# First stage in another order, adaptive columns spread over both products of the first FFN, keys stored once, spills read behind middle chunks

## The chip, the cores and the metric

The kernel runs on one core of one Trainium2 chip. The metric is the device time of one execution in microseconds. Kernel and reference work in float32. On TensorE a float32 product is made of three products of rounded float32 halves, so every product of two 128-wide tiles with 512 columns is three matmuls of 128x512.

## The reference, cut to what matters

A two-block transformer with 512 tokens and width 1024. All norms are followed by a shift and a scale that come from a conditioning vector `c` (the "adaptive" columns).

```python
ada = silu(c) @ ada_w + ada_b          # shift and scale vectors of every norm
# block A
h = modulate(rms_norm(x, pre_mix_g0), shift, scale)
x = x + gate * rms(gmlp_mixer(h, w_in, ...))      # u, v = gelu(h @ w_in), v mixed over tokens
x = x + gate * rms(swiglu(modulate(rms_norm(x)), w_gu0, w_down0))
# shared keys and values
h = modulate(rms_norm(x, kv_norm_g), *mod_kv)
k, v, f = split(h @ kv_w);  k = rms_norm(k);  dcum = cumsum(log_sigmoid(f))
# block B: mixers in one residual sum
q, gate = split(modulate(rms_norm(x)) @ w_qg)
o = softmax(q k^T / 8 + dcum[t] - dcum[s], causal) v
...                                       # further mixers: indexed attention, mLSTM
x = x + gate * rms(swiglu(modulate(rms_norm(x)), w_gu1, w_down1))
```

Token embeddings `p @ w_pl` are made at the start and used later.

## The kernel before, in words

**Split operands.** `wsplit` (L272 to L281) takes a weight tile of 128x1024 (512 KB, loaded by SP into the ring `raw` of four): ACT rounds it into `whi` (L277), then DVE or POOL subtracts it to give `wlo` (L280). `share=n` gives every n-th subtraction to POOL, 0 gives all to DVE. Activations have the same two parts, `h[0]` (high) and `h[1]` (low). `mm3` (L413 to L416) issues high times high (L414), high times low or low times high (L415, L416).

**Products.** `gemm_a` (L418) makes transposed outputs, 24 matmuls to a block: the first four blocks as a group, then block by block. `gemm_b` (L457) makes outputs with tokens in the partitions, in chunks of 256 rows of weights, 24 matmuls each, over four PSUM accumulators.

**Adaptive columns.** 96 of the 112 columns of `ada` that are needed are made in the background by `fill` (L305): it loads one column as a 128x1024 tile into the `raw` ring and lets DVE multiply and sum it in one operation (L300). One loaded column is held back. In the first FFN's gate and up product (`ffn`, L590) two columns go to each block, and what is left then follows it in a `while` loop (L608). `need` (L321) makes a vector complete before its use.

**First stage** (L616 to L776). The orders of ACT, DVE, PE and SP are written by hand in one block. It rounds `pT`, makes embeddings (`embed`, a product of 6 matmuls and an evacuation at L670 to L672), the squares of `x` (L689) and the norm of two tiles at a time (`norm2`, L685), then for each of eight column groups `prep`: two adaptive columns (L300), three small DVE operations (L729 to L731), a weight split, four transposes (L382), an ACT evacuation with scale and shift (L405), a DVE cast into the high part (L406) and a DVE subtraction into the low part (L407). `products(k)` multiplies with `w_v` chunk `k//2`, and with two blocks of `w_u`. `prep(k+1)` is written ahead of `products(k)`.

**Keys and queries.** The keys of a pair of heads (128x512) are split and written to DRAM by `spread` (L938, on POOL's queue), each half of the partitions twice, so that loads find the tiles in the form in which the logits use them: four tiles of 256 KB to a pair (`kscr`). `loader` (L944) reads them back a pair ahead, four tiles to a pair. The indexed attention has six tiles to a pair in `ascr` (`ev_a`, L1284).

**Spills.** Eight transposed tiles of normed `x` are written to DRAM earlier (`xT`) and read back at L1122 to L1129: load, ACT scale and shift (L1127), DVE cast and subtraction. This loop stands ahead of the product of `w_vv`. ACT evacuates the keys of group 1 at L886 and L889 in the same stretch; `kdone(1)` then rounds and writes them.

**Gates.** `columns` (L1249) transposes `iwt` and then, at L1259, the gates `la` and `lt` of the mLSTM, in one function that runs at the first block of `w_aqk`.

Of the kernel before, what the change touches and what calls it, by code (L numbers as in the profile page):

```python
# [20 lines left out]
P = 128  # L21
# [10 lines left out]
ND = 2  # L32
LATE = 2
AHEAD = 3
PRE = 4
# [5 lines left out]
GU = (2, 3)  # L41
GG = (1, 1)
DT = (4, 4)
DS = (0, 0)
# [3 lines left out]
IG = 1  # L48
# [141 lines left out]
def body(tc, nc, a):  # L190
    V, S_, G, PE = nc.vector, nc.scalar, nc.gpsimd, nc.tensor

    with ExitStack() as es:
# [99 lines left out]
        def ada_load(col, raw=None):  # L293
# [5 lines left out]
        def ada(col, raw):  # L299
            V.scalar_tensor_tensor(raw, raw, 1.0, cact[0], ALU.mult, ALU.mult, accum_out=modc[:, col:col + 1])  # L300
# [4 lines left out]
        def fill(n=1):  # L305

            frac[0] += n
            while frac[0] >= 1:
                frac[0] -= 1
                if ada_next[0] < len(ADA):  # L310
                    held.append(ada_load(ADA[ada_next[0]]))
# [106 lines left out]
        def gemm_a(h, w, n, evac, m=P, group=0, nfill=0, share=0, gshare=1):  # L418
# [38 lines left out]
        def gemm_b(h, w, groups, kt, evac, head=False, tail=0, nfill=0, share=0, raws=(), hshare=1, then={}):  # L457
# [6 lines left out]
            for gi in groups:  # L464
# [125 lines left out]
        def ffn(l, h, xsrc, xdst, gb, nxt):  # L590
            with tc.tile_pool(name=f"f{l}", bufs=44) as pf:
# [19 lines left out]
                gemm_b((hh, hl), a[f"w_dn{l}"], range(2), KF, post(gb, xsrc, xdst, F, nxt()), tail=DT[l], share=DS[l])  # L611
# [7 lines left out]
        accs = [acc() for _ in range(NT)]  # L619
        h = hpair()  # L620
        with tc.tile_pool(name="l0", bufs=20) as p0:
# [7 lines left out]
            EVA = (0, 0)  # L629

            crow = L2()[0:1, :]
            nc.sync.dma_start(crow, a["crow"])
            pf = [L(), L()]
            wpl = []
            for k in range(2):
                nc.sync.dma_start(pf[k], a["pT"][k])
            for k in range(2):
                wpl.append(load_w(a["w_pl"][k, 0]))
            xn = {}
            for t in range(NT):  # L640
                xn[t] = [L(), L()]
                for q in range(2):
                    nc.sync.dma_start(xn[t][q], a["x"][t * P:(t + 1) * P, q * 512:(q + 1) * 512])
                if t == 1:
                    nc.sync.dma_start(vecs[:], a["vecs"])
                    nc.sync.dma_start(ident[:], a["ident"])

            relb = L()[0:32, 0:8]
            nc.sync.dma_start(relb, a["relb"])
            oneh = L2()[0:32, 0:640]  # L650
            nc.sync.dma_start(oneh, a["onehot"])
            bscr = scratch([8, 640])
            ada0, raws = {}, {}
            for k in range(PRE):
                ada0[k] = [ada_load(col, L2()) for col in (8 + k, k)]
                if k < 4:
                    raws[k] = load_w(a["w_v"][0, k // 2] if k % 2 == 0 else a["w_u"][k // 2])
# [3 lines left out]
            ss = small()  # L661

            def embed(t, g):
                pt = tp()
                for k in range(2):
                    mm3(pt, pl[0][k][:, t * P:(t + 1) * P], pl[1][k][:, t * P:(t + 1) * P],
                        wsp[g][0][:, k * 512:(k + 1) * 512], wsp[g][1][:, k * 512:(k + 1) * 512], k == 0, k == 1)
                ple[t, g] = T()
                if g or t > 1:
                    S_.activation(ple[t, g], pt, AF.Copy)  # L670
                else:
                    V.tensor_copy(ple[t, g], pt)  # L672

            def norm2(t):

                r = ss[:, 8 + t:10 + t]
                V.reduce_sum(r, ss[:, 2 * t:2 * t + 4].rearrange("p (t q) -> p t q", t=2), AX.X)
                rsq(r, r, 1.0 / D)
                for i in range(4):
                    c = xn[t + i // 2][i % 2]  # L680
                    ri = ss[:, 8 + t + i // 2:9 + t + i // 2]
                    if t + i // 2 < 3:
                        V.tensor_scalar_mul(c, c, ri)
                    else:
                        S_.activation(c, c, AF.Copy, scale=ri)  # L685

            def squares(t):
                for q in range(2):
                    S_.activation(junk(), xn[t][q], AF.Square, accum_out=ss[:, 2 * t + q:2 * t + q + 1])  # L689
            with tc.manual_schedule(engines={mybir.EngineType.Activation, mybir.EngineType.DVE, mybir.EngineType.PE, mybir.EngineType.SP}):  # L690
                S_.activation(crow, crow, AF.Silu)

                S_.activation(junk()[:, 0:1], epsc[:], AF.Sqrt)
                for k in range(2):
# [5 lines left out]
                wsp = [wsplit(None, share=g, raw=wpl[g]) for g in range(2)]  # L700
                cact.append(tile_of(pca, "cact", n=D))
                for q in range(2):
# [3 lines left out]
                    V.tensor_copy(cact[0][:, q * 512:(q + 1) * 512], pt)  # L706
                squares(0)
                squares(1)
                embed(0, 0)
                norm2(0)  # L710
                squares(2)
                squares(3)
                embed(1, 0)
                norm2(2)
                embed(2, 0)
                embed(3, 0)
                for c0, n in ((0, 512), (512, 128)):
                    pt = tp()
                    PE.matmul(pt[0:8, 0:n], relb, oneh[:, c0:c0 + n], start=True, stop=True)
                    bt = L()[0:8, 0:n]  # L720
                    V.tensor_copy(bt, pt[0:8, 0:n])
                    bts.append((bt, c0, n))
                g0 = newg()


                def mods(j, loads):
                    for col, raw in loads:
                        ada(col, raw)
                    V.tensor_add(modc[:, j:j + 1], modc[:, j:j + 1], vc("adab", j))  # L729
                    V.scalar_tensor_tensor(g0[:, j:j + 1], modc[:, 8 + j:9 + j], 1.0, vc("adab", 8 + j), ALU.add, ALU.add)  # L730
                    V.tensor_mul(g0[:, j:j + 1], g0[:, j:j + 1], vc("pmg0", j))  # L731
                wv, uw, uaccs = {}, {}, []
                early_w = []

                def prep(k):
                    mods(k, ada0[k] if k in ada0 else [ada_load(col, L2() if k % 2 < ND else None) for col in (8 + k, k)])
                    c = k // 2
# [904 lines left out]
```

## Time and profile before

| what | value |
|---|---|
| runs, us | 1885.8, 1879.63, 1886.22 (median 1885.8) |
| own time of the profiled execution, us | 1873.39 |
| its span, us | 1871.5 |
| TensorE (PE) busy | 1822.3 us, 97% of the span |
| VectorE (DVE) busy | 60% |
| ScalarE (ACT) busy | 42% |
| GpSimd (POOL) busy | 19% |
| DMA moved | 305.76 MB, 163 GB/s over the span |

The page gives one execution, from its first to its last instruction. PE is the engine to watch, but its 97% are a mean; a matmul also counts as busy while it runs at a lower granted clock. Where PE loses time is read from windows (busy time and granted clock of a stretch) and from the list of its waits, which names the line that waited and the one that let it go.

### The profile page before, as it was taken

What the parts mean: (1) busy time and instruction counts of PE and PEld (TensorE: products, weight loads), DVE (VectorE), ACT (ScalarE), POOL (GpSimd) and SP (SyncE); (2) the same over time, 40 slices, a digit from 0 to 9 for tenths busy, and PEclk for the clock granted to TensorE, in tenths of its full rate; (3) what the DMA queues carried; (4) which work ended last, traced back from release to release, by engine and by line L of the source; (5) the groups of instructions that cost most, each with busy time, mean ns of one, the idle gap of its engine ahead of it and who ended that gap; (6) DMA issues with size and microseconds to landing.
All of it is one profiled execution on the core that took longest, in us unless ns stands there. A gap on an engine that the chain in (4) does not pass through costs nothing. (4 is left out here: it accounts for less than half of the span.)

```text
span 1871.5 us, 23902 instructions
## 1 busy us (share of the span) xinstructions
PE 1822.3 (97%) x8688; PEld 1504.1 (80%) x8688; DVE 1126.0 (60%) x2166; ACT 789.9 (42%) x1395; POOL 357.9 (19%) x294
## 2 busy tenths in 40 slices
PE   8999999999999999999999999999999999999997
PEld 5788888888777877787778888888887878888886
DVE  7869745577774256549876423332278978746534
ACT  5333324422222244558765322322256256455334
POOL 2000000222220023343331211100012562031022
PEclk9999999999999999999999999999999999999999
DMA  9674563587775437745533332332436553333532
GB/s 341 234 251 144 159 230 113 171 268 242 253 260 189 147 120 232 259 168 163 165 102 113 112 102 90 101 112 91 147 130 193 176 164 123 106 96 107 173 110 78
DMA packets 101969, 305.76 MB, mean 163 GB/s; under 512 B 12278, under 2 KB 13086, under 8 KB 101851
## 3 DMA queue, kind: packets, MB, share of 16 engines
q1 hardware_dynamic: 93402, 276.96, 44.7%
q0 software_dynamic: 8448, 27.27, 4.1%
q8 instruction: 69, 1.13, 0.2%
q14 instruction: 50, 0.40, 0.1%
HBM read 269.50 MB, written 37.30 MB: 164 GB/s over the span
## 5 line engine op out<-in xcount | busy, mean ns | idle before, releaser
L277 ACT ACTIVATE whi<-raw 128x1024 fp32r<-128x1024 f32 x281 | 296.7, 1058 | 644.2 <-PE acc L416 303.4
L280 DVE TENSOR_TENSOR wlo<-raw,whi 128x1024 fp32r<-128x1024 f32 x191 | 238.3, 1251 | 303.8 <-ACT whi L277 285.0
L414 PE MATMUL acc<-h,whi 128*128 128x512 f32 x896 | 350.5, 391 | 3.2 <-DVE t L603 2.6
L416 PE MATMUL acc<-h,wlo 128*128 128x512 f32 x896 | 349.5, 390 | 4.1 <-DVE wlo L280 4.0
L280 POOL TENSOR_TENSOR wlo<-raw,whi 128x1024 fp32r<-128x1024 f32 x90 | 221.7, 2465 | 673.0 <-ACT whi L277 593.7
L415 PE MATMUL acc<-h,whi 128*128 128x512 f32 x896 | 348.9, 389 | 0.0
L414 PE MATMUL acc<-whi,h 128*128 128x512 f32 x608 | 242.2, 399 | 8.8 <-DVE h L406 5.2
L415 PE MATMUL acc<-wlo,h 128*128 128x512 f32 x608 | 240.3, 396 | 1.4 <-POOL wlo L280 1.1
L416 PE MATMUL acc<-whi,h 128*128 128x512 f32 x608 | 240.1, 396 | 0.0
L416 PEld LDWEIGHTS acc<-h,wlo 128*128 128x128 f32 x896 | 168.2, 188 | 41.7 <-DVE wlo L280 6.6
L414 PEld LDWEIGHTS acc<-h,whi 128*128 128x128 f32 x896 | 168.3, 188 | 40.0 <-issue 5.3
L415 PEld LDWEIGHTS acc<-h,whi 128*128 128x128 f32 x896 | 168.3, 188 | 34.5
L300 DVE SCALAR_TENSOR_TENSOR raw<-raw,cact 128x1024 f32<-128x1024 f32 x96 | 146.4, 1536 | 76.7 <-DMA raw<-in_ada 73.9
L414 PE MATMUL acc<-whi,s 128*128 128x512 f32 (+1 forms) x488 | 190.6, 391 | 0.6 <-DVE t L1328 0.6
L415 PE MATMUL acc<-wlo,s 128*128 128x512 f32 (+1 forms) x488 | 190.9, 391 | 0.3 <-DVE wlo L280 0.3
L416 PE MATMUL acc<-whi,s 128*128 128x512 f32 (+1 forms) x488 | 190.2, 390 | 0.0
L414 PEld LDWEIGHTS acc<-whi,h 128*128 128x128 f32 x608 | 115.5, 190 | 33.6 <-DVE h L406 6.4
L416 PEld LDWEIGHTS acc<-whi,h 128*128 128x128 f32 x608 | 115.6, 190 | 26.0 <-DVE h L407 2.0
L415 PEld LDWEIGHTS acc<-wlo,h 128*128 128x128 f32 x608 | 115.7, 190 | 25.5 <-POOL wlo L280 1.9
L572 POOL DMA_DIRECT2D scr<-s x24 | 13.3, 556 | 541.5 <-DVE s L571 540.4
L414 PEld LDWEIGHTS acc<-whi,s 128*128 128x128 f32 x488 | 91.7, 188 | 20.4 <-DVE t L1328 1.0
L415 PEld LDWEIGHTS acc<-wlo,s 128*128 128x128 f32 x488 | 91.7, 188 | 19.3 <-DVE wlo L280 0.6
(371 smaller groups left out, 2779.4 us busy)
## 6 DMA issues: line engine op xcount, KB each, us to landing
raw<-in_ada SPq DMA_DIRECT2D x96, 512.0 KB, 4.1
raw<-in_w_gu SPq DMA_DIRECT2D x88, 512.0 KB, 4.0
raw<-in_w_dn SPq DMA_DIRECT2D x44, 512.0 KB, 3.4
scr<-t POOLq DMA_DIRECT2D x56, 256.0 KB, 5.6
raw<-in_w_o SPq DMA_DIRECT2D x20, 512.0 KB, 3.3
row<-scr SPq DMA_DIRECT2D x36, 256.0 KB, 2.7
d<-in_ada SPq DMA_DIRECT2D x16, 512.0 KB, 6.9
raw<-in_w_v SPq DMA_DIRECT2D x16, 512.0 KB, 4.7
```

The source lines that it names most:

```text
L277: S_.activation(hi[:, 0:n], raw[:, 0:n], AF.Copy)
L280: e.tensor_sub(lo[:, 0:n], raw[:, 0:n], hi[:, 0:n].bitcast(F32))
L300: V.scalar_tensor_tensor(raw, raw, 1.0, cact[0], ALU.mult, ALU.mult, accum_out=modc[:, col:col + 1])
L414: PE.matmul(out, lh, rh, start=start, stop=False)
L415: PE.matmul(out, lh, rl, start=False, stop=False)
L416: PE.matmul(out, ll, rh, start=False, stop=stop)
L572: nc.gpsimd.dma_start(xdst[rows, h * 512:(h + 1) * 512], xr[h])
```

## The change

- **First stage.** Loads come in another order (`w_pl` first, `pT`, `x`, then the rest, `w_v` and `w_u` chunks one by one). Half of the squares go to DVE, all four tiles of `x` are normed together (one reduction, one root) and ahead of everything in `products`. Four embeddings use the accumulators, three of the other four are multiplied ahead of the first transposes. A column group's high part comes from ACT straight from PSUM, its float32 form by a second ACT operation; the DVE cast goes. The DVE subtraction follows the adaptive columns of the next group. Three small DVE operations become two. `products` runs four high-high, four high-low, then four low-high matmuls. All of this stage's weight subtractions are on DVE.
- **First FFN.** All weight subtractions of its gate and up product go to DVE; 1.625 columns instead of 2 go to a block. The rest of the columns is loaded as two halves of 128x512 into the pool `H` and made behind chunks of its down product. The loop for leftovers stands in the next norm.
- **Keys and queries** are written once (2 instead of 4 tiles to a pair, 4 instead of 6). They are read by halves of 64 partitions: 8 loads instead of 4 to a pair for keys, 12 instead of 6 for the indexed attention.
- **Spills.** Three are loaded ahead of `w_vv`; ACT, cast and subtraction of two at a time stand behind chunks 1 and 2 of each group.
- **Gates.** The transposes of `la` and `lt` get a function of their own, called at the last block of `w_aqk`.
- `ND`, `PRE`, `GG`, `DS` and `IG` go, with no effect of their own.

```diff
-GU = (2, 3)
+GU = (0, 3)
@@ ada_load, ada, fill: with half, two tiles 128x512 @@
+            if half:
+                raw = [half(), half()]
+                for q in range(2):
+                    nc.sync.dma_start(raw[q], a["ada"][col][:, q * 512:(q + 1) * 512])
+                return col, raw
...
+                for q in range(2):
+                    V.scalar_tensor_tensor(raw[q], raw[q], 1.0, cact[0][:, q * 512:(q + 1) * 512], ALU.mult, ALU.mult,
+                                           accum_out=s[:, q:q + 1])
+                V.tensor_add(modc[:, col:col + 1], s[:, 0:1], s[:, 1:2])
...
-                if len(held) > 1 or ada_next[0] >= len(ADA) and held:
+                if len(held) > depth or ada_next[0] >= len(ADA) and held:
@@ gemm_b @@
-                    if 0 < c < nch - 1:
-                        fill(nfill)
+                    if 0 < c < nch - (2 if half else 1):
+                        fill(nfill, half, 3 if half else 1)
...
+                    if each:
+                        each(c)
@@ ffn @@
-                gemm_a(h, a[f"w_gu{l}"], 2 * KF, evac, group=4, nfill=2, share=GU[l], gshare=GG[l])
-                while len(done) < len(ADA):
-                    fill()
+                gemm_a(h, a[f"w_gu{l}"], 2 * KF, evac, group=4, nfill=1.625, share=GU[l])
...
+                gemm_b((hh, hl), ..., tail=DT[l], nfill=1.5, half=None if l else lambda: H(F32))
@@ first stage @@
+                for n, (l, r) in enumerate(((0, wh), (0, wl), (1, wh))):
+                    for t in range(NT):
+                        PE.matmul(accs[t], h[l][k][:, t * P:(t + 1) * P], r[:, o], ...)
...
+                squares(0)
+                squares(1, True)
+                for t in range(2):
+                    embed_out(t, 0, em[t])
+                squares(2)
+                wsp.append(wsplit(None, raw=wpl[1]))
+                squares(3, True)
+                r = ss[:, 8:12]
+                V.reduce_sum(r, ss[:, 0:8].rearrange("p (t q) -> p t q", t=NT), AX.X)
+                rsq(r, r, 1.0 / D)
...
+                for k in range(KD):
+                    f = T()
+                    S_.activation(h[0][k], pt, AF.Identity, scale=g0[:, k:k + 1], bias=modc[:, k:k + 1])
+                    S_.activation(f, pt, AF.Identity, scale=g0[:, k:k + 1], bias=modc[:, k:k + 1])
+                    if k == 0:
+                        embed_out(3, 0, em[3])
+                        embed_out(0, 1, em1[0])
+                        em1[3] = embed_mm(3, 1)
+                        for t in range(1, 3):
+                            embed_out(t, 1, em1[t])
...
+                    if k < KD - 1:
+                        for m in mod0[k + 1]:
+                            ada(*m)
+                    V.tensor_sub(h[1][k], f, h[0][k].bitcast(F32))
+                    if k < KD - 1:
+                        columns(k + 1)
+                        if k in X:
+                            split_X(k)
...
+                        pt = turned(k + 1)
                     products(k)
@@ keys and queries @@
-                    spread(kscr[pr], range(4), hi.bitcast(F32), lo.bitcast(F32))
+                    for q, part in enumerate((hi, lo)):
+                        nc.gpsimd.dma_start(kscr[pr, q], part.bitcast(F32))
...
+            return [(at[2 * hv + q], ot, d[q, me]) for hv, me in enumerate((TOP, BOT)) for q in range(2) for ot in (TOP, BOT)]
@@ spills @@
-            for j in range(KD):
-                f = T()
-                nc.sync.dma_start(f, xT[j])
-                S_.activation(f, f, AF.Identity, scale=gm[:, j:j + 1], bias=sm[:, j:j + 1])
-                V.tensor_copy(hx[0][j], f)
-                V.tensor_sub(hx[1][j], f, hx[0][j].bitcast(F32))
+            def unspill(c):
+                if c in (0, 3):
+                    return
+                for _ in range(2):
+                    j = len(hdone)
+                    hdone.append(j)
+                    f = spilled[j]
+                    S_.activation(f, f, AF.Identity, scale=gm[:, j:j + 1], bias=sm[:, j:j + 1])
+                    V.tensor_copy(hx[0][j], f)
+                    V.tensor_sub(hx[1][j], f, hx[0][j].bitcast(F32))
+                    if len(spilled) < KD:
+                        spill_load()
...
+            for _ in range(3):
+                spill_load()
             gemm_b(hk, a["w_vv"], range(2), KD, lambda g, t, pt: vsplit(g, t, pt, va, vdone),
-                   then={0: lambda: kdone(1)})
+                   then={0: lambda: kdone(1)}, each=unspill)
@@ gates @@
                 if i == 0:
                     columns()
+                if i == 3:
+                    gates_T()
```

ACT at the start of the first stage, where the first column group's high part is made; before, L670 is an embedding's evacuation, L277 a weight's high part, L405 a column group's evacuation:

```order
L277 ACTIVATE whi_280<-raw_152 128x1024
L670 ACTIVATE t_291<-tp_284 128x512
L670 ACTIVATE t_300<-tp_293 128x512
L405 ACTIVATE t_307<-tp_302,modc,gcol 128x512
L670 ACTIVATE t_318<-tp_311 128x512
L670 ACTIVATE t_327<-tp_320 128x512
L277 ACTIVATE d_334<-raw_158 128x1024
L405 ACTIVATE t_343<-tp_338,modc,gcol 128x512
```

and with the change, where L768 scales a half tile of `x`, L676 is an embedding, L272 a weight, L786 and L787 are the column group's high part and its float32 form:

```order
L768 ACTIVATE s_124<-s_124,sm_111 128x512
L768 ACTIVATE s_128<-s_128,sm_111 128x512
L768 ACTIVATE s_125<-s_125,sm_111 128x512
L768 ACTIVATE s_129<-s_129,sm_111 128x512
L676 ACTIVATE t_251<-acc_201 128x512
L272 ACTIVATE whi_253<-raw_148 128x1024
L786 ACTIVATE h_92<-tp_278,modc,gcol 128x512
L787 ACTIVATE t_289<-tp_278,modc,gcol 128x512
L676 ACTIVATE t_292<-acc_208 128x512
L676 ACTIVATE t_294<-tp_257 128x512
L676 ACTIVATE t_303<-tp_264 128x512
L676 ACTIVATE t_305<-tp_271 128x512
```

The first column group now stands behind the scaling of `x`, and three evacuations of embeddings stand between it and the second group.

DVE in the middle of the first FFN's gate and up product before; L300 is an adaptive column, L280 a weight's low part, L603 the product of gate and up, L548 its low part:

```order
L300 SCALAR_TENSOR_TENSOR raw_3540,modc<-raw_3540,cact_194 128x1024
L300 SCALAR_TENSOR_TENSOR raw_3543,modc<-raw_3543,cact_194 128x1024
L280 TENSOR_TENSOR wlo_3536<-raw_3533,whi_3535 128x1024
L300 SCALAR_TENSOR_TENSOR raw_3579,modc<-raw_3579,cact_194 128x1024
L300 SCALAR_TENSOR_TENSOR raw_3582,modc<-raw_3582,cact_194 128x1024
L603 TENSOR_TENSOR t_3407<-t_3407,acc_3415 128x512
L548 TENSOR_TENSOR s_3448<-t_3407,s_3447 128x512
L300 SCALAR_TENSOR_TENSOR raw_3621,modc<-raw_3621,cact_194 128x1024
```

and with the change (L307, L275, L613, L558 in the same order):

```order
L307 SCALAR_TENSOR_TENSOR raw_3670,modc<-raw_3670,cact_180 128x1024
L558 TENSOR_TENSOR s_3503<-t_3462,s_3502 128x512
L275 TENSOR_TENSOR wlo_3624<-raw_3621,whi_3623 128x1024
L307 SCALAR_TENSOR_TENSOR raw_3673,modc<-raw_3673,cact_180 128x1024
L275 TENSOR_TENSOR wlo_3666<-raw_3663,whi_3665 128x1024
L307 SCALAR_TENSOR_TENSOR raw_3709,modc<-raw_3709,cact_180 128x1024
L307 SCALAR_TENSOR_TENSOR raw_3748,modc<-raw_3748,cact_180 128x1024
L613 TENSOR_TENSOR t_3540<-t_3540,acc_3548 128x512
L275 TENSOR_TENSOR wlo_3705<-raw_3702,whi_3704 128x1024
L558 TENSOR_TENSOR s_3581<-t_3540,s_3580 128x512
L307 SCALAR_TENSOR_TENSOR raw_3751,modc<-raw_3751,cact_180 128x1024
```

Each block now has one weight subtraction on DVE, and between one and two columns instead of two.

ACT where the spilled columns meet the evacuations of the keys of group 1, before (L1127 is a spilled column, L886 and L889 evacuate keys):

```order
L1127 ACTIVATE t_5799<-t_5799,modc,gcol 128x512
L886 ACTIVATE gb_5705<-acc_5528 128x512
L889 ACTIVATE k_5707<-acc_5528 128x512
L886 ACTIVATE gb_5705<-acc_5529 128x512
L889 ACTIVATE k_5711<-acc_5529 128x512
L1127 ACTIVATE t_5804<-t_5804,modc,gcol 128x512
L886 ACTIVATE gb_5705<-acc_5530 128x512
L889 ACTIVATE k_5715<-acc_5530 128x512
L1127 ACTIVATE t_5809<-t_5809,modc,gcol 128x512
L886 ACTIVATE gb_5705<-acc_5531 128x512
```

and with the change (L1192, L940, L943):

```order
L1192 ACTIVATE t_5842<-t_5842,modc,gcol 128x512
L1192 ACTIVATE t_5844<-t_5844,modc,gcol 128x512
L272 ACTIVATE whi_5854<-raw_5852 128x1024
L1192 ACTIVATE t_5846<-t_5846,modc,gcol 128x512
L272 ACTIVATE whi_5928<-raw_5926 128x1024
L940 ACTIVATE gb_5763<-acc_5594 128x512
L943 ACTIVATE k_5765<-acc_5594 128x512
L940 ACTIVATE gb_5763<-acc_5595 128x512
L943 ACTIVATE k_5769<-acc_5595 128x512
L940 ACTIVATE gb_5763<-acc_5596 128x512
```

Before, four of the eight spilled columns stand ahead of the evacuations and two between them; now three stand ahead and none between. The other five follow further on, behind the rounding of these keys and ahead of the values of the first group of `w_vv`.

## Rows read from the trace of the kernel before

**Rows 1.** Page, part 1: busy time, share, instructions of each engine.
```profile
PE 1822.3 (97%) x8688; PEld 1504.1 (80%) x8688; DVE 1126.0 (60%) x2166; ACT 789.9 (42%) x1395; POOL 357.9 (19%) x294
```

**Rows 2.** Waits of PE, whole span: line, waited for, us in total, times, longest.
```profile
PE acc L414 <- DVE h L406: 5.2, 4, 2.2
PE acc L416 <- DVE wlo L280: 4.0, 5, 1.0
PE acc L414 <- ACT k L889: 3.5, 1, 3.5
...
PE tp L1259 <- DVE t L1269: 2.2, 1, 2.2
```

**Rows 3.** Windows: busy us and instructions of each engine, granted clock, DMA share, GB/s.
```profile
core 0: us, PE busy (x) PEld busy (x) DVE busy (x) ACT busy (x) POOL busy (x), PEclk, DMA share, GB/s
0.00:72.09 72.09, 60.83 (x232) 44.03 (x233) 55.01 (x105) 34.09 (x53) 12.50 (x9) 0.95 0.82 301
38.00:41.30 3.30, 3.30 (x10) 2.53 (x9) 3.23 (x9) 1.19 (x2) 0.00 (x0) 0.50 1.03 392
480.00:576.00 96.00, 88.88 (x376) 68.92 (x375) 73.79 (x96) 26.13 (x34) 16.80 (x7) 1.00 0.79 260
576.00:680.00 104.00, 104.00 (x461) 86.00 (x460) 28.94 (x30) 25.18 (x33) 0.34 (x1) 1.00 0.39 131
746.00:760.00 14.00, 10.46 (x35) 7.28 (x34) 10.46 (x20) 11.21 (x19) 0.00 (x0) 0.76 0.70 243
751.30:758.10 6.80, 5.74 (x14) 4.49 (x15) 6.29 (x12) 6.80 (x15) 0.00 (x0) 0.50 0.79 277
```

**Rows 4.** Timeline of PE: start, us, instruction, idle before and releaser; first and last product.
```profile
25.59 0.48 PE L414 MATMUL acc<-whi,h 128*128 128x512 f32 x1
...
36.58 0.50 PE L414 MATMUL acc<-whi,h 128*128 128x512 f32 x1 [1.92 <-DVE h L406]
...
72.09 0.39 PE L414 MATMUL acc<-whi,h 128*128 128x512 f32 x1
```

**Rows 5.** Timeline of DVE, first stage.
```profile
27.93 1.23 DVE L280 TENSOR_TENSOR d<-raw,d 128x1024 fp32r<-128x1024 f32 x1
...
30.13 3.43 DVE L300 SCALAR_TENSOR_TENSOR d<-d,cact 128x1024 f32<-128x1024 f32 x1
...
33.49 1.21 DVE L300 SCALAR_TENSOR_TENSOR d<-d,cact 128x1024 f32<-128x1024 f32 x1
```

**Rows 6.** Timeline of POOL, the same stretch.
```profile
29.92 2.55 POOL L280 TENSOR_TENSOR wlo<-raw,whi 128x1024 fp32r<-128x1024 f32 x1 [5.67 <-ACT whi L277]
```

**Rows 7.** Timeline of ACT, first stage.
```profile
15.74 0.63 ACT L689 ACTIVATE junk<-s 128x512 bf16<-128x512 f32 x1
...
17.21 1.33 ACT L685 ACTIVATE s<-s,sm 128x512 f32<-128x512 f32 x2 [0.23 <-DVE sm L358]
...
25.43 0.60 ACT L670 ACTIVATE t<-tp 128x512 f32<-128x512 f32 x1 [0.77 <-PE tp L416]
...
28.12 0.78 ACT L405 ACTIVATE t<-tp,modc,gcol 128x512 f32<-128x512 f32 x1 [1.14 <-DVE gcol L731]
```

**Rows 8.** Lines of DVE by form, 480 to 566: busy us, mean ns, idle before, releaser.
```profile
L300 DVE SCALAR_TENSOR_TENSOR raw<-raw,cact 128x1024 f32<-128x1024 f32 x29 | 49.2, 1713 | 16.4 <-DMA raw<-in_ada 16.3
...
L603 DVE TENSOR_TENSOR t<-t,acc 128x512 f32<-128x512 f32 x7 | 4.8, 680 | 0.0
```

**Rows 9.** Timeline of ACT at the spilled columns.
```profile
744.01 0.82 ACT L1127 ACTIVATE t<-t,modc,gcol 128x512 f32<-128x512 f32 x1 [8.61 <-DMA t<-scr]
```

**Rows 10.** Timeline of PE at the gates' transposes.
```profile
1421.39 0.41 PE L1259 MATMUL tp<-ident,t 4*128 4x4 f32 x4 [2.21 <-DVE t L1269]
```

**Rows 11.** Source L990 (first matmul of an attention's logits): durations, first and last start.
```profile
L990 PE MATMUL tp<-k,qk x64: 277/362/468, 832.0 to 965.5; 128*128 128x256 f32 x32, 128*128 128x384 f32 x16, 128*128 128x512 f32 x16
...
L990 PE MATMUL tp<-qk,qk x32: 280/335/393, 1510.3 to 1573.4; 128*128 128x256 f32 x16, 128*128 128x384 f32 x8, 128*128 128x512 f32 x8
```

**Rows 12.** DMA issues: shape, count, KB, median us from issue to landing.
```profile
k<-scr SPq DMA_DIRECT2D x32, 256.0 KB, 4.5
```

More of the change, by code (lines that the diff above doesn't have):

```diff
@@ L299, in ada @@
         def ada(col, raw):
+            if isinstance(raw, list):
+                s = small()
+                for q in range(2):
[3 more added lines that the diff above has]
+                return
             V.scalar_tensor_tensor(raw, raw, 1.0, cact[0], ALU.mult, ALU.mult, accum_out=modc[:, col:col + 1])
@@ L303, in body, with fill @@
         frac = [0.0]
-        def fill(n=1):
+        def fill(n=1, half=None, depth=1):
             frac[0] += n
@@ L455, in gemm_a, with gemm_b @@
                 i += len(run)
-        def gemm_b(h, w, groups, kt, evac, head=False, tail=0, nfill=0, share=0, raws=(), hshare=1, then={}):
+        def gemm_b(h, w, groups, kt, evac, head=False, tail=0, nfill=0, share=0, raws=(), hshare=1, then={}, each=None, half=None):
             hi, lo = h
@@ L618, in body @@
         plscr = scratch([NT, 2, P, 512])
-        accs = [acc() for _ in range(NT)]
+        accs = []
         h = hpair()
@@ new lines, in columns, with turned, products @@
+            def columns(k):
+                V.scalar_tensor_tensor(g0[:, k:k + 1], modc[:, 8 + k:9 + k], ab1[:, k:k + 1], vc("pmg0", k), ALU.add, ALU.mult)
+                V.tensor_add(modc[:, k:k + 1], modc[:, k:k + 1], vc("adab", k))
+            def turned(k):
+                pt = tp()
+                for t in range(NT):
+                    PE.transpose(pt[:, t * P:(t + 1) * P], xn[t][k // 4][:, (k % 4) * P:(k % 4 + 1) * P], ident[:])
+                return pt
+            def products(k):
+                c, kk = k // 2, k % 2
+                (wh, wl), o = wv[c], slice((k % 2) * 512, (k % 2 + 1) * 512)
+                for n, (l, r) in enumerate(((0, wh), (0, wl), (1, wh))):
+                    for t in range(NT):
+                        PE.matmul(accs[t], h[l][k][:, t * P:(t + 1) * P], r[:, o], start=k == n == 0, stop=k == KD - 1 and n == 2)
+                for q in range(min(NU, (k + 1) // 2)):
+                    wh, wl = uw[q]
+                    if k == 2 * q + 1:
+                        uaccs.append(tp())
+                    for k_ in range(0 if k == 2 * q + 1 else k, k + 1):
+                        mm3(uaccs[q], wh[:, k_ * P:(k_ + 1) * P], wl[:, k_ * P:(k_ + 1) * P], h[0][k_], h[1][k_],
+                            k_ == 0, k_ == KD - 1)
@@ L713, in body @@
[L713 to L731, printed above, removed]
@@ new lines, in body @@
+                squares(3, True)
+                r = ss[:, 8:12]
+                V.reduce_sum(r, ss[:, 0:8].rearrange("p (t q) -> p t q", t=NT), AX.X)
+                rsq(r, r, 1.0 / D)
+                for q in range(2):
+                    for t in range(NT):
+                        c, ri = xn[t][q], ss[:, 8 + t:9 + t]
+                        if t < 2:
+                            S_.activation(c, c, AF.Copy, scale=ri)
+                        else:
+                            V.tensor_scalar_mul(c, c, ri)
@@ L869, in nxt0, with mod @@
         def nxt0():
-            hk.extend(hpair())
-            return halves(hk, lambda: (gain(104, "kvg"), need(96)), xT)
+            def mod():
+                while len(done) < len(ADA):
+                    fill()
+                hk.extend(hpair())
+                return gain(104, "kvg"), need(96)
+            return halves(hk, mod, xT)
         ffn(0, hf, xs[1], xs[2], lambda: gb_row(40, "qfg0"), nxt0)
@@ L1241, in ev_ix @@
                     V.tensor_scalar_add(gt[0][64:128], pt[64:128], vc("bgate", 0)[64:128, :])
[L1242 removed]
+            gemm_a(h, a["w_ix"], 5, ev_ix, group=4)
             g = gt[0]
```

244 lines of the change are left out of this document (119 added, 125 removed).

## The prediction

> **What bounds the kernel now.** I read the page's first part, then what PE waits for, then windows of the places that came up, and only there the other engines. The first says that PE works for 97% of the span [rows 1]. So the end can only come earlier where PE stands still or runs at a low clock. The list of PE's waits [rows 2] names four that this change touches: high parts of the first stage (5.2 us in 4), low parts of weights from DVE (4.0 in 5), an evacuation of keys (3.5 in 1) and a small tile ahead of the gates' transposes (2.2 in 1). The windows [rows 3] show what these places cost in all. The measure is the stretch 576 to 680, where PE never stands: 104.0 us for 461 matmuls, 0.2256 us from one 128x512 matmul to the next. Each other window's matmuls times this is what it would need without loss.
>
> **First stage.** From the first product at 25.59 to the first of the next weight at 72.09 [rows 4] it takes 46.5 us. It holds 144 product matmuls of 0.2256, 32.5 us, and seven groups of transposes that I put at some 0.36 each, 2.5: 35.0. So 11.5 us are lost. A wait of 1.92 at 36.58 [rows 4] is of the kind listed for the high part [rows 2]. Its cause stands in three rows: DVE's column operation at 30.13 takes 3.43 us, while the same at 33.49 takes 1.21 [rows 5], and the long one runs beside POOL's subtraction of 29.92 to 32.47 [rows 6]. The high part stands behind it on DVE. Behind the wait PE runs at a granted clock of 0.50, the lower of its two levels, for 3.3 us [rows 3], which costs half of that, 1.65.
>
> The change takes POOL away (its 2.55 become 1.23 on DVE [rows 5, 6]), takes the cast off DVE and lets ACT make the high part. DVE then needs, per column group, two columns at 1.21 and a small end, some 1.3 each, a weight's low part at 1.23 in six of the groups, a subtraction of some 0.7 and two small operations: under 5 us, against 35.6/8 = 4.5 of PE in the mean, and it begins some 5 us ahead of PE. I take PE as the bound from its first product on.
>
> That product, though, starts later. Squares are two at 0.76 for a tile [rows 7], so half of them on DVE saves ACT some 3 us; but the order puts the root of all four tiles behind an embedding's evacuations, a weight's high part and its subtraction on DVE (1.23), then two squares of DVE, about 0.75 each by the nearest row. By this chain all of `x` is normed at some 21.5 (four scalings on ACT at 1.33 for two [rows 7]), the first two columns follow on DVE to 24, then ACT's two operations of 0.78 and two evacuations of 0.60 [rows 7] to 27, then on PE an embedding that waits for the second evacuation, 6 matmuls or 1.4, and four transposes: 29. Before, it was 25.59. Bounds are 26 (loads and squares off the chain) and 32 (the matmuls of the embeddings at half clock). The work from there is 35.0 and 0.6 for two small products that move in: 35.6, so 64.6. PE stands still ahead of it, and some of the low clock will remain; I take 1.5 such stretches of 1.65, 2.5, between none and two. The next weight begins at 67.1. Gain: 72.1 − 67.1 = **5.0**, between 10.5 (26 + 35.6, no low clock) and 0 (a start at 32 with two low stretches is still 1.2, and I allow one wait more).
>
> **First FFN, gate and up.** The window 480 to 576 has 376 matmuls, 84.8 us: 11.2 are lost, of 88.9 counted as busy [rows 3]. DVE makes columns there: 29 in 86 us at a mean of 1.71, against 1.21 alone, and it stands still for 16.4 us before them, for their loads [rows 8]. It is this order, columns ahead of the next low part, that PE's 4.0 us on low parts come from, and POOL's work stretches the columns as in the first stage. With the change a block has on DVE 1.625 columns at 1.3 (2.1), a subtraction (1.23), a product at 0.68 [rows 8] and its low part at about the same: 4.7 us against 24 matmuls, 5.41. What remains open is the wait for loads: 16.4/29 = 0.57 for a column, 0.92 for a block, and 5.6 in all if none of it goes: 0.2 over, 3.3 us in 15.7 blocks. I take half of that as left, 1.7, and a gain of **9.5**, between 11.2 and 4. The lower end is worked out from the loads: a block needs 2.625 tiles of 0.524 MB, 1.376 MB; at today's 260 GB/s [rows 3] that is 5.3 us, just covered; at a tenth less it is 5.9, 7 us over the window.
>
> The 16 columns left for the down product, and ACT's part, cost nothing: DVE is busy there for 28.9 of 104 us [rows 3] and gets some 26 more (16 times two halves and an addition), the loads add 8.4 MB to 131 GB/s, 80 GB/s. If that cover fails, it is one low part late, some 2 us.
>
> **Spills and keys.** In 746 to 760 PE works for 10.5 of 14 us, and from 751.3 to 758.1 at the lower clock: 3.5 us of standing and half of 5.74, 2.9 [rows 3]: 6.4. The wait behind it is the 3.5 us for a key's evacuation [rows 2]. ACT stood 8.61 us for a spilled tile until 744.01 [rows 9], and the evacuations stand behind these in its order. Now three spills are ahead of them, loaded early; the last of them ends before the accumulators are full. The other five read tiles that come free only when the rounded keys are in DRAM, and stand ahead of the values' evacuation; I leave 0.9 for that: gain **5.5**, between 6.4 and 0 (the values then wait as the keys did).
>
> Keys and queries: POOL has half of its issues, and fewer bytes are written. The loads keep their bytes, 1 MB for a pair of heads. A tile takes 4.5 us from issue to landing [rows 12], and the eight pairs of the first attention take 133.5 us, 16.7 each (832.0 to 965.5), the four of the second 63.2, 15.8 each [rows 11]. Loads run a pair ahead. So I cost this at nothing; twice as many loads of half the size must exceed 16.7 us before anything waits. The Trainium skill ("DMA: Bandwidth & Descriptors", section "Rules for kernel authors") advises against two transfers to disjoint halves of the partitions, since both use the same engines and serialize; by it a half tile may take as long as a whole one, and the time would be that of the last rival. No row here shows a half tile of a key.
>
> **Gates.** PE waited 2.21 us at 1421.39, and 0.34 behind it [rows 10]. The transposes now come three blocks later, when the tile is long there. Gain **2.0**, between 2.5 and 0.
>
> **The sum.** 5.0 + 9.5 + 5.5 + 2.0 = 22.0. The profiled execution took 1873.4; so 1851.4 on its scale. It lies 12.4 below the median of the runs, 1885.8, and the runs lie up to 6.6 apart. On the scale of the median I predict 1863.8, rounded to **1864**.
>
> **Rivals.**
> *The columns' loads still bound gate and up.* For it: DVE stands for loads, not for work, in 16.4 of 86 us, and the ring of four stays. Against: a fifth fewer columns. The gain there is 4, the time 1885.8 − 16.5 = 1869. Chance 0.13.
> *The first stage gives nothing.* For it: the later start and PE's low clock behind a pause. Against: the waits for DVE are gone in any case. 1885.8 − 17 = 1869. Chance 0.12.
> *Several places lose their gain together*, the values waiting in place of the keys the most likely (ACT's order has four spills ahead of them): 22 − 5.5 − 5.0 − 4 and so about 8 left, 1878, within what counts as the same. This is also the case in which the change does not do what it says. Chance 0.09.
> *Slower: half tiles come late.* If a half tile takes the 4.5 us of a whole one and only two are under way at a time, eight take 18 us against 16.7, and twelve 27 against 15.8: 8 × 1.3 + 4 × 11.2 = 55 us lost, 1885.8 − 22 + 55 = 1919. With three at a time (12 and 18) only the second attention loses, 9 us. It decides from about 2 us for a half tile in the mean. Against it: a half tile is half the bytes, and the mean rate over the span is 163 GB/s, 1 MB in 6 us. Chance 0.04.
>
> **How the numbers follow.** The forecast has 0.62. Range: all terms at their upper bounds give 30.6 (10.5 + 11.2 + 6.4 + 2.5), 1855, and the fastest run before lies 6 below the median: 1849 at the low end. At the high end gains of 9 (0 + 4 + 3 + 2), 1877. A measurement of this kernel can tell about 0.5%, 9.4 us. Faster by more holds the forecast and the first two rivals, 0.87, less 0.01 for their tails: 0.86; the same 0.10; slower 0.04.
>
> **What would show it.** The first product near 29 and the next weight near 67; no wait of PE for high parts of over 1 us there, and no column operation of over 3 us. 480 to 560 with PE busy throughout and DVE near its limit, without POOL. No wait for an evacuation of keys at 750, and none for the values 20 us later. No wait ahead of the gates' transposes. Wrong it would be if DVE or its loads still held low parts in gate and up, or if waits stood in the attention before a key tile.

## The result, and the profile after

| | before | changed |
|---|---|---|
| median of 4 runs, us | 1882.7 (1878.15 to 1886.22) | 1860.7 (1858.07 to 1867.28) |
| span of the profiled execution, us | 1871.5 | 1856.6 |

The changed kernel takes 0.9891 of the time before, with a 95% interval of 0.9866 to 0.9916: 20.5 us faster by the ratio, 22.0 by the medians. The two profiled spans lie only 14.9 apart; the execution profiled before (1873.4) is faster than any of its runs shown. What follows is about those 14.9, since only the traces say where time goes. That the sum of the prediction, 22.0, is the difference of the medians is partly luck, as its terms will show.

First the page and the waits of PE after the change, in the columns of [rows 1] and [rows 2]:

```profile
PE 1816.7 (98%) x8688; PEld 1508.0 (81%) x8688; DVE 1106.1 (60%) x2222; ACT 797.2 (43%) x1402; POOL 274.6 (15%) x237
```

```profile
PE tp L389 <- DVE t L375: 5.8, 1, 5.8
PE tp L750 <- ACT d L737: 3.3, 1, 3.3
PE tp L421 <- ACT t L787: 3.2, 1, 3.2
PE acc L421 <- DVE v L960: 2.8, 1, 2.8
PE tp L1379 <- ACT t L1382: 2.5, 2, 1.8
```

The four waits of [rows 2] are gone. Three have come or grown: 5.8 us for a normed tile ahead of its transposes (L389; 0.7 before), 2.8 for the values' evacuation (L960), 2.5 for the scores of the indexed attention (L1382). The 3.2 us (L787) stand ahead of the first product. The windows show the places:

```profile
core 0: us, PE busy (x) PEld busy (x) DVE busy (x) ACT busy (x) POOL busy (x), PEclk, DMA share, GB/s
0.00:66.09 66.09, 57.21 (x233) 43.07 (x233) 47.60 (x96) 39.68 (x59) 0.20 (x4) 0.97 0.93 343
470.00:565.00 95.00, 95.00 (x421) 78.55 (x421) 64.65 (x109) 26.99 (x35) 0.00 (x0) 1.00 0.75 249
736.00:750.00 14.00, 14.00 (x72) 11.74 (x71) 11.27 (x16) 9.57 (x13) 3.25 (x6) 1.00 0.74 247
750.00:764.00 14.00, 11.16 (x48) 8.94 (x47) 9.41 (x19) 6.72 (x13) 2.30 (x3) 0.96 0.91 324
1400.00:1418.00 18.00, 15.45 (x65) 13.33 (x64) 13.93 (x25) 11.26 (x21) 2.17 (x4) 0.81 0.55 173
```

Gate and up (470 to 565) runs without a loss, 421 matmuls in 95.0 us, 0.2256 each. The keys' evacuations (736 to 750) hold nothing any more; the 14 us behind them lose 2.8. At the scores (1400 to 1418) PE now stands and falls to a mean clock of 0.81.

Both traces hold 8688 matmuls, so the start of the n-th in one can be set against the n-th in the other. By that, with stretches in us of the trace after:

| stretch | change, us | predicted |
|---|---|---|
| first stage, 0 to 66 | −6.0 | −5.0 |
| first FFN, 479 to 588 | −11.4 | −9.5 |
| its norm and the first keys, 678 to 716 | +5.3 | none |
| spills, keys, values, 728 to 776 | −2.6 | −5.5 |
| gates and scores, 1398 to 1432 | +3.2 | −2.0 |
| behind PE's last matmul | −2.6 | none |
| all else | −0.8 | 0 |
| sum | −14.9 | −22.0 |

The places where the first stage's two ends stand, answering to [rows 4] (timeline of PE):

```profile
27.46 1.84 PE L703 MATMUL acc<-whi,h 128*128 128x512 f32 x4
...
66.09 0.39 PE L421 MATMUL acc<-whi,h 128*128 128x512 f32 x1
```

The first product starts 1.9 us later than before, the first product with the next weight ("the next weight" from here on) 6.0 earlier.

### The profile page after: what moved, and what is told of

It is laid out like the page before. It is cut to its first block, busy times and chain, and to the rows that moved or that the text cites. A ratio compares the mean times of both kernels' runs of the same rounds, so it can differ in the third digit from the quotient of the medians.

```text
span 1856.6 us, 24000 instructions
## 1 busy us (share of the span) xinstructions
PE 1816.7 (98%) x8688; PEld 1508.0 (81%) x8688; DVE 1106.1 (60%) x2222; ACT 797.2 (43%) x1402; POOL 274.6 (15%) x237
## 4 chain that ended last, share of the span: by engine, by line
PE 87%; DVE 7%; ACT 3%; issue 2%; DMA 1%; POOL 0%; SPq 0%; DVEq 0%; ACTq 0%; POOLq 0%
PE acc L421 25%; PE acc L423 25%; PE acc L422 25%; PE tp L1085 1%; PE acc L703 1%; PE tp L1070 1%; PE tp L389 1%; PE acc L458 1%; PE acc L453 1%; PE acc L452 1%; PE tp L886 1%; PE tp L1043 1%; PE tp L1044 1%; DVE wlo L275 1%; PE tp L421 1%
## 5 line engine op out<-in xcount | busy, mean ns | idle before, releaser
L272 ACT ACTIVATE whi<-raw 128x1024 fp32r<-128x1024 f32 x281 | 296.8, 1059 | 654.5 <-PE acc L423 299.7
L275 DVE TENSOR_TENSOR wlo<-raw,whi 128x1024 fp32r<-128x1024 f32 x216 | 268.6, 1246 | 302.2 <-ACT whi L272 282.6
L421 PE MATMUL acc<-whi,h 128*128 128x512 f32 x576 | 227.7, 396 | 2.8 <-DVE v L960 2.8
L422 PE MATMUL acc<-wlo,h 128*128 128x512 f32 x576 | 226.5, 393 | 0.3 <-DVE wlo L275 0.3
L423 PE MATMUL acc<-whi,h 128*128 128x512 f32 x576 | 226.5, 394 | 0.0
L275 POOL TENSOR_TENSOR wlo<-raw,whi 128x1024 fp32r<-128x1024 f32 x65 | 157.8, 2429 | 452.6 <-ACT whi L272 402.8
L421 PE MATMUL acc<-whi,s 128*128 128x512 f32 (+1 forms) x496 | 194.4, 392 | 0.9 <-ACT cact L752 0.8
L423 PE MATMUL acc<-whi,s 128*128 128x512 f32 (+1 forms) x496 | 194.1, 391 | 0.0
L307 DVE SCALAR_TENSOR_TENSOR raw<-raw,cact 128x1024 f32<-128x1024 f32 x80 | 97.7, 1223 | 96.8 <-DMA raw<-in_ada 96.6
L421 PEld LDWEIGHTS acc<-whi,h 128*128 128x128 f32 x576 | 109.0, 189 | 25.6 <-ACT v L958 3.2
L422 PEld LDWEIGHTS acc<-wlo,h 128*128 128x128 f32 x576 | 109.0, 189 | 22.5 <-DVE wlo L275 0.7
L423 PEld LDWEIGHTS acc<-whi,h 128*128 128x128 f32 x576 | 108.9, 189 | 22.0
```

Source lines behind the costliest of these rows:

```text
L272: S_.activation(hi[:, 0:n], raw[:, 0:n], AF.Copy)
L275: e.tensor_sub(lo[:, 0:n], raw[:, 0:n], hi[:, 0:n].bitcast(F32))
L421: PE.matmul(out, lh, rh, start=start, stop=False)
L422: PE.matmul(out, lh, rl, start=False, stop=False)
L423: PE.matmul(out, ll, rh, start=False, stop=stop)
```

## The experiments

Each kernel is the changed one with one edit (i_all and i_ds join three), timed against the kernel before on the same chip (whose medians were 1879 to 1880 there). By its ratio the changed kernel would stand there at 1858.6 to 1859.5.

| run | median, us | ratio, 95% interval | span, us |
|---|---|---|---|
| u_first | 1865.5 | 0.9926 (0.9910 to 0.9943) | 1865.0 |
| p_first | 1862.8 | 0.9907 (0.9878 to 0.9936) | 1860.8 |
| b_first | 1861.1 | 0.9905 (0.9884 to 0.9926) | 1860.3 |
| f_rate | 1867.2 | 0.9943 (0.9926 to 0.9960) | 1863.0 |
| f_gu | 1860.0 | 0.9900 (0.9877 to 0.9923) | 1858.4 |
| i_order | 1853.9 | 0.9865 (0.9844 to 0.9886) | 1849.9 |
| u_spill | 1858.8 | 0.9894 (0.9878 to 0.9909) | 1856.5 |
| u_keys | 1876.4 | 0.9984 (0.9973 to 0.9994) | 1874.8 |
| i_spill | 1856.3 | 0.9881 (0.9858 to 0.9903) | 1854.2 |
| u_gates | 1861.1 | 0.9907 (0.9892 to 0.9922) | 1858.6 |
| i_all | 1849.2 | 0.9843 (0.9821 to 0.9864) | 1846.2 |
| i_ds | 1850.8 | 0.9849 (0.9828 to 0.9870) | 1847.1 |

### First stage: order, or POOL?

**u_first** puts the whole stage back.

> The changed kernel with the first stage as it was before (order of loads, normalisation in pairs, cast on DVE, low parts on POOL). Theory: the first weight of the second group starts at 72.1 again instead of 66.1, the rest keeps its distances, so about 6 us more than the changed kernel, 1866.5. Rival: the stage's gain is lost again further on, at a wait that comes at a fixed time, and the total stays at 1861.

The next weight started at 74.4, 8.3 us later than 66.1. That is also 2.3 later than in the trace before, whose first stage is the same, so two traces of one stage can differ by that much. The span is 8.4 longer: 8.3 here, 2.0 in gate and up, 1.6 at the values and 1.9 further on, less 5.4 that this build gets back at 680, where its order of PE is that of before (see i_order).

**p_first** keeps the new order and gives POOL five low parts.

```diff
-                    wv[c] = wsplit(None, raw=raws[k])
+                    wv[c] = wsplit(None, share=1, raw=raws[k])
...
-                wsp.append(wsplit(None, raw=wpl[1]))
+                wsp.append(wsplit(None, share=1, raw=wpl[1]))
```

> The changed kernel with POOL taking five low parts of weights in the first stage again (the four of the values' weight and one of the embeddings'). Theory (POOL beside DVE stretches the columns from 1.2 to 3.4 us, and that was what held the high parts): columns of 3.4 us in the first stage, the next weight 3 to 6 us later than 66.1; 680 comes out as before in this kernel, which gives 5 back. Total 1858 to 1862. Rival (the order and the high part on ACT alone made the gain, DVE has time enough): the next weight still at 66.1, total 1855.5.

The next weight came at 73.4: all of the gain was gone. (680 gave 5.4 back, so the span is only 4.2 longer.) The timelines of POOL and DVE, and the wait of PE:

```profile
31.65 2.92 POOL L275 TENSOR_TENSOR wlo<-raw,whi 128x1024 fp32r<-128x1024 f32 x1 [8.57 <-ACT whi L272]
```

```profile
31.12 1.22 DVE L307 SCALAR_TENSOR_TENSOR d<-d,cact 128x1024 f32<-128x1024 f32 x1
...
32.26 2.85 DVE L798 TENSOR_TENSOR h<-t,h 128x512 fp32r<-128x512 f32 x1
```

```profile
PE acc L703 <- DVE h L798: 4.0, 2, 2.1
```

Here POOL's subtraction (31.65 to 34.57) hits not a column but the low part of `h`, 2.85 us where one without POOL beside it takes 0.69, and PE waits for it.

**b_first** is the other half: the stage as before, all low parts on DVE (`share=0` at its two splits).

> The changed kernel with the first stage as before the change, except that all of its low parts of weights are made on DVE. Theory (what held the stage was POOL beside DVE, and the new order is not what pays): the next weight starts between 64 and 68, close to the changed kernel's 66.1, total near 1861. Rival (DVE has too much with its cast and the late high part, so the order is needed too): the next weight at 69 to 72, 3 to 6 us more.

The next weight came at 65.3, 0.8 earlier than with the new order and 9.1 earlier than in u_first, from which it differs by these two splits alone. DVE's columns by form, in u_first and here (lines of DVE, 0 to 74: count, busy us, mean ns):

```profile
L309 DVE SCALAR_TENSOR_TENSOR d<-d,cact 128x1024 f32<-128x1024 f32 x16 | 25.5, 1629 | 0.0
```

```profile
L309 DVE SCALAR_TENSOR_TENSOR d<-d,cact 128x1024 f32<-128x1024 f32 x16 | 18.9, 1218 | 0.0
```

So the stage's gain is five subtractions moved from POOL to DVE. The new order, the cast that went and the two ACT operations gave nothing that these traces show. The total of b_first is no better, since this build lost 3.2 us in gate and up and 1.8 at the values, in code that the edit leaves alone. u_first, u_keys and i_all lose 2.0 to 2.2 in gate and up too, without an edit in common; no run here has a reason.

### First FFN: POOL, or the rate of the columns?

**f_rate** has `GU = (2, 3)` again, with 1.625 columns to a block.

> The changed kernel, but POOL takes every second low part of a weight in the first FFN's gate and up product again (20 subtractions); 1.625 columns to a block and the columns in the down product stay. Theory (POOL beside DVE is what stretched the columns): column operations of 3.4 us come back, the stretch from 480 on loses 8 to 11 us against the changed kernel; the order of PE at 680 is that of before again, which gives 5 back: 1864 to 1867. Rival (fewer columns to a block are what gave the gain): the stretch keeps its 11 us, and with the order at 680 the total is 1855.

Gate and up took 11.6 us more than in the changed kernel, 680 gave 5.4 back, the values took 1.9, the first stage and the gates gave 2.1; with smaller differences the span is 6.4 longer. Lines of DVE by form, f_rate from 440 to 567 and the changed kernel in the same stretch:

```profile
L307 DVE SCALAR_TENSOR_TENSOR raw<-raw,cact 128x1024 f32<-128x1024 f32 x32 | 55.7, 1741 | 39.2 <-DMA raw<-in_ada 36.4 <-issue 2.8
```

```profile
L307 DVE SCALAR_TENSOR_TENSOR raw<-raw,cact 128x1024 f32<-128x1024 f32 x29 | 35.5, 1222 | 36.2 <-DMA raw<-in_ada 36.2
```

The wait for the columns' loads is the same 36 us in both; the column's mean is not. **f_gu** has two columns to a block again, none in the down product, and no POOL.

> The changed kernel with two columns to a block in the gate and up product again and none in the down product, all low parts on DVE. Theory (POOL is the cause, the rate is not): DVE needs 2 x 1.3 + 1.2 + 1.4 = 5.2 us in a block against 5.4 of PE, the stretch 480 to 565 stays without loss, total 1861 within 2. Rival (the lower rate is needed): PE waits for low parts again, 3 to 6 us more.

Through this stretch its distance from the changed kernel moves by less than 0.1 us. The lower rate and the halves in the down product gave nothing; POOL is the whole gain.

### The new wait at 680

PE's order is set by a scheduler that the kernel doesn't write out there. In the changed kernel the second pair's transposes stand 20 matmuls earlier than before, ahead of products that were ready; DVE has the normed tiles at the same distance in both. **i_order** is a small edit that turns the order back.

```diff
-GU = (0, 3)
+GU = (41, 3)
```

> The changed kernel with one or two of the subtractions of the first FFN's gate and up product back on POOL (every 41st of all weights). It does nearly nothing by itself, but the order of PE at 680 comes out as before: the second pair's transposes stand 20 matmuls later. Theory (the 6 us wait of PE at 680 is a matter of that order alone): 5.3 us less than the changed kernel, all of it between 675 and 716; 1855.5. Rival (PE waits for DVE there in any order): no difference, 1861.

5.4 us came back between 677 and 716, and the wait shrank to 0.6. All 14 traces agree: seven have the order of the changed kernel here and wait 5.8 us, seven have that of before and wait 0.6 to 0.7.

```profile
PE tp L389 <- DVE t L375: 0.6, 1, 0.6
```

### Spills and keys

**u_spill** reads all eight spilled tiles ahead of the values' product, as before.

> The changed kernel with all eight spilled tiles read ahead of the product of values, as before. Theory: the wait of 3.5 us for a key's evacuation and the low clock behind it come back and the wait of 2.8 us before the second group of values goes: 2 to 4 us more than the changed kernel in 720 to 790, 1863 to 1865. Rival: both waits are for the same DMA of the keys and cost the same, total unchanged.

It lost 4.7 us up to 749 and got 4.6 back by 776: nothing in sum, as the rival said. **u_keys** leaves the spills late and writes keys and queries twice again (`kscr` of 4 and `ascr` of 6 tiles, `spread`, whole tiles read).

> The changed kernel with keys and queries written twice and read in whole tiles, as before. Theory (costs nothing either way in the attention; the shorter writes let the spilled tiles come earlier): the attention keeps its time, the wait ahead of the second group of values grows from 2.8 to 4 to 6 us, total 1 to 3 us more. Rival (half tiles come later than whole ones): 2 to 5 us less, between 830 and 960 and between 1495 and 1560.

Far more than either: 4.6 us up to 749 and 8.7 from there to 776, 13.3 in all, and 1876.4 in total. Its waits of PE, and ACT and POOL in the stretch:

```profile
PE acc L421 <- DVE v L960: 11.1, 1, 11.1
```

```profile
769.31 0.81 ACT L1197 ACTIVATE t<-t,modc,gcol 128x512 f32<-128x512 f32 x1 [12.16 <-DMA t<-scr]
```

```profile
751.30 0.60 POOL L995 DMA_DIRECT2D scr<-t  x1 [20.37 <-ACT t L1141]
...
765.32 0.61 POOL L995 DMA_DIRECT2D scr<-t  x1 [0.89 <-DMA scr<-t]
```

POOL issues sixteen writes from 751.3 to 765.9; a spilled tile's buffer comes free only when its key is in DRAM, and ACT stands 12.2 us for it with the values' evacuation behind. In the changed kernel the eight writes of this group end at 751.8 (issue) and ACT stands 4.5. So over 728 to 776, against the changed kernel: late and written once 0.0, early and once 0.1, early and twice (the kernel before) 2.6, late and twice 13.3. By these corners what this part gained is the single write; the new place of the spills is worth nothing with it and costs 10.7 without. Only the 13.3 is clear of the spread, though: u_first, b_first, f_rate and u_gates, which leave this stretch alone, lose 1.6 to 2.5 us more in it than the changed kernel, and the kernel before lacks the other edits as well. So the 10.7 is shown, the gain of 2.6 is argued.

In the attentions themselves nothing moved: the half tiles land in 3.5 us where whole ones took 4.5 [rows 12], and the first attention lasts 133.6 us (133.5 in [rows 11]), the second 63.0 (63.2):

```profile
k<-scr SPq DMA_DIRECT2D x64, 128.0 KB, 3.5
```

```profile
L1043 PE MATMUL tp<-k,qk x64: 277/364/468, 817.1 to 950.7; 128*128 128x256 f32 x32, 128*128 128x384 f32 x16, 128*128 128x512 f32 x16
...
L1043 PE MATMUL tp<-qk,qk x32: 278/337/396, 1498.5 to 1561.5; 128*128 128x256 f32 x16, 128*128 128x384 f32 x8, 128*128 128x512 f32 x8
```

**i_spill** loads the spilled tiles into the values' buffers.

```diff
-                spilled.append(T())
-                nc.sync.dma_start(spilled[-1], xT[len(spilled) - 1])
+            for j in range(KD):
+                spilled.append(tile_of(px, "v", bufs=8))
+                nc.sync.dma_start(spilled[j], xT[j])
```

> The changed kernel with the eight spilled tiles loaded into buffers of the values, which are free by then, so that no load waits for the keys' DMA. Theory (the wait of 2.8 us ahead of the second group of values is for the spilled tiles that wait for that DMA): the wait and the restart behind it go, 3 us less than the changed kernel between 750 and 780. Rival (eight spilled columns in a row on ACT hold the evacuations of the first group of keys): a wait of 2 to 5 us near 695 to 710 in its place, no gain.

Both hold in part: 4.5 us less between 749 and 776, 3.0 more between 677 and 716, where seven of them stand in a row on ACT. The span is 2.4 shorter, not the 3 of the theory, nor the rival's nothing. Windows of i_spill:

```profile
695.00:720.00 25.00, 22.46 (x104) 17.74 (x103) 22.40 (x43) 15.84 (x26) 2.31 (x4) 1.00 0.59 191
745.00:780.00 35.00, 35.00 (x159) 28.83 (x158) 13.03 (x27) 13.89 (x21) 12.43 (x13) 1.00 0.60 204
```

### Gates

**u_gates** puts the transposes of `la` and `lt` back into `columns()`.

> The changed kernel with the gates' transposes back at the first block of queries and keys of the indexed attention. Theory: the wait of 2.2 us for the gates comes back, but the later waits for the scores' evacuations (1.8 and 0.7) and the low clock behind them go: 3 us less than the changed kernel in 1395 to 1450, 1857.5. Rival: the two waits have nothing to do with each other, and it is 2 us slower, 1863.

From 1398 to 1432 it was 3.2 us shorter, with 0.6 given back up to 1480. The same matmuls in u_gates and in the changed kernel (windows):

```profile
1400.30:1431.00 30.70, 28.14 (x138) 23.40 (x138) 26.20 (x47) 21.53 (x39) 3.63 (x7) 1.00 0.49 160
1398.00:1432.00 34.00, 31.45 (x138) 26.30 (x138) 27.02 (x48) 22.73 (x39) 3.79 (x7) 0.90 0.47 152
```

PE stands for 2.6 us in either. The waits of PE, in u_gates for the gates and just behind them, in the changed kernel for the scores, and one of ACT there for a scan of DVE (L1333):

```profile
1408.70 0.40 PE L1329 MATMUL tp<-ident,t 4*128 4x4 f32 x4 [2.22 <-DVE t L1339]
1409.45 0.36 PE L1374 MATMUL tp<-s,s 128*128 128x256 f32 x1 [0.35 <-issue]
```

```profile
1410.46 0.38 PE L1379 MATMUL tp<-s,s 128*128 128x256 f32 x1 [1.79 <-ACT t L1382]
1411.94 0.58 PE L1379 MATMUL tp<-s,s 128*128 128x256 f32 x1 [0.74 <-ACT t L1382]
1407.74 0.38 ACT L1382 ACTIVATE t<-tp 128x256 f32<-128x256 f32 x1 [1.60 <-DVE t L1333]
```

The kernel before has 1.00 and 30.8 us there. So the wait has only moved, and what the changed kernel lost is the lower granted clock, 0.90 in the mean. That is not settled by this edit alone: of the ten builds with the late transposes one has 1.00 there and the others 0.90 to 0.95, of the four with the early ones three have 1.00 and i_ds 0.95. The total doesn't show the 3.2 (1861.1): the wait for the values grew from 2.8 to 4.7 us in its profile and a stretch near 1768 by 1.9, both in code that the edit leaves alone.

### A faster version

**i_all** joins i_order, i_spill and u_gates.

> Order at 680 as before, spilled tiles in the values' buffers and the gates' transposes at the first block, together. Theory (the three waits are independent): 5.3 + 3 + 3 us less than the changed kernel, 1849. Rival (one of them is taken over by the next wait): 1853 to 1856.

1849.2, 0.9843 of before. Against the changed kernel 4.9 came back from 677 to 716, 4.5 from 728 to 776, 3.0 at the gates; 2.0 were lost in gate and up, where PE waited 1.7 us for DVE. **i_ds** turns the order with POOL in the down product instead (`share=0 if l else 8`, `GU = (0, 3)`).

> As the kernel with all three mendings, but the order at 680 comes from giving every eighth low part of the down product to POOL, where DVE has time, and none in gate and up. Theory: the 2 us that the mended kernel lost in gate and up come back, 1847. Rival (POOL beside DVE costs as much in the down product): 1849 or more.

The 2.0 us did come back in gate and up, but the gates' stretch gave 1.8 where it had given 3.0, and 1.5 went before 1512. 1850.8 is the same as i_all, and the theory's 1847 did not come. Nor is it shown that POOL's subtraction cost those 2.0 us: i_order has the same edit and loses nothing in gate and up, u_keys has none there and loses 2.2. Both kernels are some 9 us faster than the changed one by the medians, 10 by the spans.

## Why the prediction was right, and where it was not

**First stage.** 5.0 were forecast and 6.0 came; first product at 27.5 against 29, next weight at 66.1 against 67.1. The mechanism, POOL beside DVE, is shown by p_first and b_first. The later start was seen rightly, and the new order pays for it, but b_first shows that neither was needed: the old order with its earlier start does as well once POOL is out. The Trainium skill ("SBUF — State Buffer", section "Who interferes with whom") says that a DVE instruction with two operands in SBUF contends with a GpSimd instruction that reads SBUF. The rows agree: 3.43 against 1.21 us [rows 5, 6], means of 1741 against 1222 ns in f_rate and the changed kernel.

**Gate and up.** 9.5 were forecast, 11.4 came, just over the upper end of 11.2. The sum held 1.7 back for the waits for loads; these stayed and cost PE nothing (f_gu, with more columns still, loses nothing either). The rival that loads bind falls.

**Spills and keys.** The failed step is "So I cost this at nothing" of the keys, beside "gain 5.5" for the spills. The range of the spills was open down to 0, for this very reason ("tiles that come free only when the rounded keys are in DRAM"), but the text didn't join the two: fewer writes are what lets these tiles come early (late spills with the double writes cost 13.3). 2.6 came; that all of it is the single write is argued from the corners. The sign "none for the values 20 us later" failed, with 2.8 us. The rival of late half tiles fell: a half tile took 3.5 us, and 3.7 in the second attention (median from issue to landing). By that twelve, two at a time, would need 22 us against 15.8 (an estimate in the rival's own terms), and the second attention kept its 63.0. The Trainium skill ("DMA: Bandwidth & Descriptors", section "Rules for kernel authors") says that two transfers to disjoint halves of the partitions serialize on the same engines. Half the bytes did take 3.5 us, not half of 4.5; whether two halves serialize no run here shows, and no wait came of it.

**Gates.** The tile was long there, as forecast, and the wait for it went. The failed step is "Gain 2.0": it took the removed wait for a gain and left out what PE does next. The scores that now come first are evacuated by ACT behind the same scans of DVE, so PE stands as long as before (2.6 us), and in this trace its granted clock fell after that. 2.0 was forecast, −3.2 came.

**Left out.** The wait of 5.8 us at 680 stood in no step, though the order of the instructions was there to compare. And the 2.6 us behind the last matmul: see below. With all terms the profile gives 14.9, where 22.0 was forecast; the executions of one kernel lie up to 9 us apart, and the medians happen to show all 22.

## What to carry to other kernels

Ask of each engine that "helps" what it holds up while it helps: 25 subtractions on the idle POOL cost PE 17 us, because the DVE operations beside them became three to four times as long (3.43 against 1.21 us, 2.85 against 0.69). A wait that is removed may only move: look at what the engine does next, and at its clock there. A buffer that is handed from a write to a read ties two edits together; price them as a pair, in all four corners. And where a scheduler sets the order, compare PE's order over the whole program, also where nothing was edited: one flipped group cost 5 us here.

## What the runs showed of the hardware that was not expected

The end of the program follows the number of POOL's DMAs. From the start of PE's last matmul to the end of the span it took 10.7 us before and in u_keys (112 DMAs from POOL), and 8.1 in the changed kernel and in the other runs that write keys once (80 DMAs). The last matmuls of before and after (timeline of PE) against spans of 1871.5 and 1856.6:

```profile
1860.83 0.28 PE L416 MATMUL tp<-whi,s 128*128 128x256 f32 x1
```

```profile
1848.51 0.28 PE L423 MATMUL tp<-whi,s 128*128 128x256 f32 x1
```

After POOL's last operation its sequencer shows nothing for 9.29 us where there were 112 DMAs (both traces) and for 6.67 where there were 80 (all twelve), 0.083 us for each DMA in either. The other engines end only after it: before, SP's last record but the closing ones ends at 1868.0 and POOL goes on at 1870.8; with the change these are 1855.7 and 1855.9. That POOL spends this time on its DMAs is inferred from the two counts; no run changed the count alone.
